# Moving the conditioning pieces, the row sums and the wide sums between the units of a one-core decoder block

## The chip, the cores and the metric

One core of one Trainium2 chip runs the whole program. The metric is the device time of one execution in microseconds (us). Matmuls run on TensorE (PE, with its weight loads shown as PEld), elementwise work on VectorE (DVE), activations and copies on ScalarE (ACT), a little on GpSimd (POOL); all transfers from memory are issued by SyncE (SP).

## The reference, cut to what matters

```
mod = silu(c) @ w_ada + b_ada;  shift, scale, gate = split(mod, 3)
h = rms_norm(x, norm1_w) * (1 + scale) + shift            # 256 tokens x 2048
q,k | v | o | z | i,f | u | B | C | zb | gA | gB = split(h @ w_in + b_in)
h_a = rms_norm(sigmoid(o) * mlstm(q, k, v, i, f)) * silu(z);   y_a = h_a @ w_proj_a
h_b = B * conv3(C * u) * silu(zb);                             y_b = h_b @ w_proj_b
x = x + gate * ((sigmoid(gA) * y_a + sigmoid(gB) * y_b) @ w_out)
out = rms_norm(x, normf_w)
```

Everything is float32; a product is made of three matmuls of a rounded head and a rest of each operand (two for the weights' rest against the head of h alone in the "wide" columns).

## The kernel before, in words

All weights stream through the core once. They are cut into 418 **units** of 128 x 1024 floats (512 KB). For each unit SP loads a tile `raw`, ACT copies its head to `wh` (L288), DVE subtracts to get the rest `wl` (L294), and PE multiplies `wh` and `wl` with the head and the rest of h. The main loop over units (L863 on) runs `advance(n + 2)` first, so DVE's instruction `wl` of unit n + 2 stands before whatever unit n adds to DVE's queue; there are three `wh` and three `wl` tiles, so ACT's copy for unit n + 2 can start only when PE is through with unit n - 1.

Units 0 to 159 are the **outer** units. h is not ready at the start, so the block goes through the five outputs qk, v, o, z, gA in **visits** (`SEGMENTS`, some k of the 16 blocks of h at a time): qk in units 0-1, v 2-3, o 4-7, z 8-13, gA 14-23, then second visits v 24-35, o 36-49, qk 50-79, z 80-105, and third or last ones o 106-119, v 120-137, gA 138-159. A unit with an even number fills one half of the output (two PSUM tiles with tag `g`), the next the other half (tag `a`). At the end of a visit `outer_evac` empties the tiles: on a first visit ACT copies them, later DVE adds them to what stands in SBUF (L394 for v, o, z; L383 for qk and gA), two adds for a half. The next visit writes the same tiles, so its first unit waits for the two adds of one half and its second for those of the other. Units 160-161 are the input and forget gates, 162-193 gB, 194-321 u, C, B, zb in four column groups j (8 units each; "wide" in all of zb and in u, C, B for j > 0: PSUM tiles are double buffered there, PE does not wait for their sums), 322-385 the two projections, 386-417 the output projection.

h itself comes from 96 **pieces** of w_ada of 512 KB each, for the matrix product with silu(c), done on DVE (L247, `ada_piece`): 64 pieces for scale and shift, then 32 for the gate. After every fourth of the first 64, four small DVE operations (L255 to L258) and one on ACT and one on DVE (L241, L242) make one more block of h. `stream` is the written order of units and pieces: piece n goes before unit u as soon as `at[n] <= u` (or when h is needed). `ADA` gives the pieces for each unit: 0.82 for the first 64, 0.45 for the rest. DVE's queue and SP's queue follow that order.

Small work that has no place of its own goes into `fillers`, of which one is run at the end of each unit. After the last visit of v, o or z its row sums are put there: `row_op` adds the bias row (L417), with `row_load` (a DMA of two 512 KB tiles) as a filler of the output before. After z's fillers (which end with the load of o's row) o's come at once.

Of the kernel before, what the change touches and what calls it, by code (L numbers as in the profile page):

```python
# [19 lines left out]
AF = mybir.ActivationFunctionType  # L20
ALU = mybir.AluOpType
PSUM = bass.MemoryType.PSUM

S, D, NH, DK, DV = 256, 2048, 8, 128, 256
# [12 lines left out]
SEGMENTS = [("qk", 0, 1), ("v", 0, 1), ("o", 0, 2), ("z", 0, 3), ("gA", 0, 5), ("v", 1, 7), ("o", 2, 9),  # L37
            ("qk", 1, 16), ("z", 3, 16), ("o", 9, 16), ("v", 7, 16), ("gA", 5, 16)]

ADA = (2.0, 0.82, 0.45)  # L40
FEATURE = ("qk", "gA")
KEEP = 4
WARM = (9, 16)
# [47 lines left out]
def body(ctx: ExitStack, tc: tile.TileContext, wu, wa, xT_d, x_d, cols_d, rows_d, out_d):  # L91
# [50 lines left out]
    pieces = [(part, k, half) for k in range(16) for part in (1, 0) for half in range(2)]  # L142
    pieces += [(2, k, half) for k in range(16) for half in range(2)]
    stream = []
    at = [0.0] * 4
    for n in range(4, len(pieces)):
        at.append(ADA[0] if n == 4 else at[-1] + 1.0 / ADA[1 if pieces[n][0] < 2 else 2])
    nxt = 0
    for u in range(NU):
        v = max(u - HD, 0)  # L150
# [198 lines left out]
    fillers = deque()  # L349
# [79 lines left out]
    def outer_after(grp, last_visit):  # L429
        if not last_visit:  # L430
            return
        d = dest[grp]
        if grp in FEATURE:
            def biased(b):
                def go():
                    for i in (b, b + 1):
                        act.activation(d[:, i, :], d[:, i, :], AF.Sigmoid if grp == "gA" else AF.Identity, bias=col(grp, i))
                return go
            if grp == "qk":
                fillers.append(row_load("z"))  # L440
            (later if grp == "gA" else fillers).extend([biased(b) for b in range(0, 16, 2)])
            return
        parts = row_op(grp, grp, ALU.add)
        if grp == "v":
            vL = {}
            vH = slot("s2", [128, 2, NH, VW], "vH", F32R)
            ml["v"] = vH, vL

            def v_split(t, half):
                hs = slice(4 * half, 4 * half + 4)  # L450

                def go():
                    act.activation(vH[:, t, hs, :], d[:, t, hs, :], AF.Copy)
                    vL[t, half] = wp.tile([128, 4, VW], F32R, name=f"vL{t}{half}", tag="ada", bufs=AB)
                    dve.tensor_tensor(vL[t, half], d[:, t, hs, :], vH[:, t, hs, :].bitcast(F32), op=ALU.subtract)
                return go
            splits = [v_split(t, half) for half in range(2) for t in range(2)]
            fillers.extend(parts[:2] + [idle] + parts[2:] + [idle] + splits)
        elif grp == "o":
            for f in parts:  # L460
                fillers.extend([f, idle])
            fillers.append(row_load("v"))
            fillers.extend(activate(d.rearrange("p t (a n) -> p (t a) n", a=2), AF.Sigmoid))
        elif grp == "z":
            for f in parts:
                fillers.extend([f, idle])
            fillers.append(row_load("hn"))
            fillers.extend(activate(d.rearrange("p t (a n) -> p (t a) n", a=2), AF.Silu))
            for f in row_op("z", "hn", ALU.mult):
                fillers.extend([f, idle])  # L470
            fillers.append(row_load("o"))
# [199 lines left out]
    def wide_sum(d, grp, j, tiles):  # L671

        for b in range(4):
            act.activation(d[:, b, :], tiles[b // 2][:, b % 2, 0:S], AF.Identity, bias=col(grp, 4 * j + b))
        for i in range(2):
            dd = d[:, 2 * i:2 * i + 2, :]
            dve.tensor_tensor(dd, tiles[i][:, :, S:2 * S], dd, op=ALU.add)

    def wide_evac(grp, j, tiles):
        u, y = hb["cv"][:, 0], hb["cv"][:, 1]  # L680
        if grp == "C":
            cu = wp.tile([128, 4, S + 4], F32, name=f"cu{j}", tag="bc", bufs=2)
            pool.memset(cu[:, :, 0:4:2], 0.0)
            wide_sum(cu[:, :, 4:], grp, j, tiles)
            dve.tensor_tensor(cu[:, :, 4:], cu[:, :, 4:], u, op=ALU.mult)
            conv_fillers(cu, j)
            return
        wide_sum(u, grp, j, tiles)
        if grp == "B":
            dve.tensor_tensor(y, u, y, op=ALU.mult)  # L690
        elif grp == "zb":
            act.activation(u, u, AF.Silu)
            zb_fillers(j)

    def conv_fillers(cu, j):
        y = hb["cv"][:, 1]
        dve.tensor_copy(cu[:, :, 1:4:2], cu[:, :, S:S + 4:2])

        def conv(b):
            def go():  # L700
                dve.tensor_scalar(y[:, b, :], cu[:, b, 0:S], col("cw0", 4 * j + b), None, op0=ALU.mult)
                dve.scalar_tensor_tensor(y[:, b, :], cu[:, b, 2:S + 2], col("cw1", 4 * j + b), y[:, b, :],
                                         op0=ALU.mult, op1=ALU.add)
                dve.scalar_tensor_tensor(y[:, b, :], cu[:, b, 4:S + 4], col("cw2", 4 * j + b), y[:, b, :],
                                         op0=ALU.mult, op1=ALU.add)
            return go
        fillers.extend([conv(b) for b in range(4)])
# [17 lines left out]
    def inner_evac(grp, j, p):  # L725
        if is_wide(grp, j):
            wide_evac(grp, j, p)
            return
        p = p[0]
        pv = p.rearrange("p a (b n) -> p (a b) n", b=2)  # L730
        blocks = [4 * j + b for b in range(4)]
        js = slice(4 * j, 4 * j + 4)
        if grp == "gB":
            if j == 0:
                hb["g"] = slot("s4", [128, 16, S], "gB")
            g = hb["g"][:, js, :]
            for b in range(4):
                act.activation(g[:, b, :], pv[:, b, :], AF.Identity, bias=col("gB", blocks[b]))
        elif grp == "u":
            if j == 0:  # L740
                hb["cv"] = slot("cb", [128, 2, 4, S], "conv_tmp")
            u = hb["cv"][:, 0]
            for b in range(4):
                act.activation(u[:, b, :], pv[:, b, :], AF.Identity, bias=col("u", blocks[b]))
        elif grp == "C":
            cu = wp.tile([128, 4, S + 4], F32, name=f"cu{j}", tag="bc", bufs=2)
            u = hb["cv"][:, 0]
            pool.memset(cu[:, :, 0:4:2], 0.0)
            for b in range(4):
                dve.scalar_tensor_tensor(cu[:, b, 4:], pv[:, b, :], col("C", blocks[b]), u[:, b, :],  # L750
                                         op0=ALU.add, op1=ALU.mult)
            conv_fillers(cu, j)
        elif grp == "B":
            y = hb["cv"][:, 1]
            for b in range(4):
                dve.scalar_tensor_tensor(y[:, b, :], pv[:, b, :], col("B", blocks[b]), y[:, b, :],
                                         op0=ALU.add, op1=ALU.mult)
        elif grp == "yA":
            g = dest["gA"][:, js, :]
            dve.tensor_tensor(g, pv, g, op=ALU.mult)  # L760
        elif grp == "yB":
            g = hb["g"][:, js, :]
            dve.tensor_tensor(g, pv, g, op=ALU.mult)
            if j == 0:
                m = slot("s01", [128, 2, 16, S], "m", F32R)
                hb["mH"], hb["mL"] = m[:, 0], m[:, 1]
            a = dest["gA"][:, js, :]

            def merge():
                dve.tensor_tensor(g, g, a, op=ALU.add)  # L770

            def merge_split():
                act.activation(hb["mH"][:, js, :], g, AF.Copy)
                dve.tensor_tensor(hb["mL"][:, js, :], g, hb["mH"][:, js, :].bitcast(F32), op=ALU.subtract)
            fillers.extend([merge, merge_split])
# [87 lines left out]
    for n, (kind, grp, k, half) in enumerate(UNITS):  # L863
# [42 lines left out]
        elif kind == "inner":  # L906
# [10 lines left out]
            if half == 7:  # L917
                while fillers and grp == "u" and k == 0 and ml["started"] < NH:
                    run_fillers(1)
                if grp == "B" or (grp == "u" and k > 0):  # L920
                    run_fillers(len(fillers))
                if grp == "yA" and k == 0:
                    run_fillers(len(fillers) + len(later))
                inner_evac(grp, k, cur["g"])
                if grp == "gB" and k == 3:
                    for j in range(4):
                        gv = hb["g"][:, 4 * j:4 * j + 4, :]
                        later.append(lambda gv=gv: act.activation(gv, gv, AF.Sigmoid))
                if grp == "yA" and k == 2:
                    fillers.append(gate_broadcast)  # L930
# [97 lines left out]
```

## Time and the profile before

| what | value |
|---|---|
| median of three runs | 1175.53 us (1174.04 to 1175.81) |
| the profiled execution, device time | 1175.07 us |
| its span, first to last instruction | 1172.6 us |
| PE busy | 1148.4 us, 98% of the span |
| DVE, ACT busy | 824.7 us (70%), 584.9 us (50%) |
| granted TensorE clock, mean | 0.998 of 2.4 GHz |

The span leaves 2.5 us of the device time outside. PE is never long idle; what it loses lies in single waits, so the timeline of PE around the ends of visits tells more than the shares.

### The profile page before, as it was taken

To read this page: it belongs to the slowest core of one execution; us is meant where nothing else is said; L and a number is where in the kernel's file an instruction comes from. 1 tells how busy PE (TensorE), PEld (TensorE's weight loads), DVE (VectorE), ACT (ScalarE), POOL (GpSimd) and SP (SyncE) were. 2 spreads that over 40 slices of the span, in tenths; PEclk is the share of its full clock that TensorE was granted. 3 is DMA by queue.
4 is the path that set the end of the run, shared out by engine and by line. 5 is a ranking of instruction groups with operands and counts; after the bars stand their busy time and mean duration, and the time that the engine had idled before them with its cause. 6 is when DMAs were issued, how large, how long until landed. Compare 5 with 4: busy or idle time off the path is not lost.

```text
span 1172.6 us, 19514 instructions
## 1 busy us (share of the span) xinstructions
PE 1148.4 (98%) x7906; PEld 1074.4 (92%) x7906; DVE 824.7 (70%) x1008; ACT 584.9 (50%) x698; POOL 16.6 (1%) x26
## 2 busy tenths in 40 slices
PE   8999999999999999999999999999999999999996
PEld 7898889988888999999999899899999999999995
DVE  6989998876888966665587566666665655556466
ACT  6754344464353556445456744644544544444453
POOL 0000000000000000000000000000000000000003
PEclk9999999999999999999999999999999999999999
DMA  9999899888788855544547556656556555486662
GB/s 345 402 368 366 317 370 360 311 323 298 260 321 295 316 199 196 182 161 161 163 163 270 197 175 222 196 180 221 194 180 227 200 195 186 144 294 208 227 206 72
DMA packets 79900, 283.48 MB, mean 242 GB/s; under 512 B 10689, under 2 KB 10817, under 8 KB 79425
## 3 DMA queue, kind: packets, MB, share of 16 engines
q1 hardware_dynamic: 79810, 282.23, 68.8%
q8 instruction: 62, 1.02, 0.3%
q14 instruction: 28, 0.23, 0.1%
HBM read 280.09 MB, written 2.11 MB: 241 GB/s over the span
## 4 chain that ended last, share of the span: by engine, by line
PE 78%; DVE 5%; ACT 2%; issue 1%; DMA 1%; DVEq 0%; ACTq 0%
PE qk L322 7%; PE out L345 6%; PE z L345 5%; PE gA L322 5%; PE v L345 3%; PE o L345 2%; PE gB2g L322 2%; PE gB1g L322 2%; PE gB3g L322 2%; PE u0g L322 2%; PE yB3g L322 2%; PE yA3g L322 2%; PE yB2g L322 2%; PE yA2g L322 2%; PE yB1g L322 2%; PE yA1g L322 2%
## 5 line engine op out<-in xcount | busy, mean ns | idle before, releaser
L294 DVE TENSOR_TENSOR wl<-raw,wh 128x1024 fp32r<-128x1024 f32 x408 | 494.8, 1222 | 272.9 <-ACT wh L288 270.5
L288 ACT ACTIVATE wh<-raw 128x1024 fp32r<-128x1024 f32 x409 | 430.4, 1059 | 444.2 <-PE qk L322 44.2
L247 DVE SCALAR_TENSOR_TENSOR ada<-ada,c_b 128x1024 f32<-128x1024 f32 x96 | 116.8, 1217 | 1.7 <-DMA ada<-wa 1.7
L345 PE MATMUL o<-wh,h 128*128 128x512 f32 x256 | 66.7, 380 | 2.2 <-DVE v_ext L394 1.6
L345 PE MATMUL v<-wh,h 128*128 128x512 f32 x256 | 66.4, 379 | 1.5 <-DVE o L394 1.5
L322 PE MATMUL qk<-h,wh 128*128 128x256 f32 x512 | 63.3, 276 | 3.9 <-DVE o L394 2.4
L345 PE MATMUL z<-wh,h 128*128 128x512 f32 x256 | 66.0, 379 | 0.0
L322 PEld LDWEIGHTS qk<-h,wh 128*128 128x128 f32 x512 | 60.0, 192 | 5.0 <-ACT h L241 1.7
L322 PE MATMUL gA<-h,wh 128*128 128x256 f32 x512 | 63.0, 276 | 0.5 <-DVE v_ext L394 0.5
L322 PEld LDWEIGHTS gA<-h,wh 128*128 128x128 f32 x512 | 60.0, 192 | 1.1 <-DVE v_ext L394 0.9
L345 PEld LDWEIGHTS o<-wh,h 128*128 128x128 f32 x256 | 48.1, 189 | 10.1 <-ACT wh L288 2.0
L345 PEld LDWEIGHTS v<-wh,h 128*128 128x128 f32 x256 | 48.2, 189 | 8.6 <-ACT wh L288 1.9
L345 PEld LDWEIGHTS z<-wh,h 128*128 128x128 f32 x256 | 48.3, 189 | 6.8
L345 PE MATMUL out<-wh,m 128*128 128x512 f32 x192 | 49.5, 379 | 0.0
L345 PEld LDWEIGHTS out<-wh,m 128*128 128x128 f32 x192 | 37.7, 197 | 3.6
L345 PE MATMUL v<-wl,h 128*128 128x512 f32 x128 | 38.2, 380 | 1.7 <-DVE wl L294 1.7
L345 PE MATMUL o<-wl,h 128*128 128x512 f32 x128 | 38.2, 380 | 0.0
L345 PE MATMUL z<-wl,h 128*128 128x512 f32 x128 | 38.1, 379 | 0.0
L322 PE MATMUL gA<-h,wl 128*128 128x256 f32 x256 | 33.8, 275 | 0.0
L322 PE MATMUL qk<-h,wl 128*128 128x256 f32 x256 | 33.8, 275 | 0.0
L322 PEld LDWEIGHTS gA<-h,wl 128*128 128x128 f32 x256 | 31.2, 192 | 0.0
L322 PEld LDWEIGHTS qk<-h,wl 128*128 128x128 f32 x256 | 31.2, 192 | 0.0
(429 smaller groups left out, 2207.2 us busy)
## 6 DMA issues: line engine op xcount, KB each, us to landing
raw<-wu SPq DMA_DIRECT2D x418, 512.0 KB, 4.4
ada<-wa SPq DMA_DIRECT2D x96, 512.0 KB, 6.0
xT<-xT SPq DMA_DIRECT2D x4, 512.0 KB, 6.3
x_res<-x SPq DMA_DIRECT2D x1, 2048.0 KB, 8.4
out<-r SPq DMA_DIRECT2D x8, 256.0 KB, 3.0
z<-rows SPq DMA_DIRECT2D x2, 512.0 KB, 7.1
hn<-rows SPq DMA_DIRECT2D x2, 512.0 KB, 8.1
o<-rows SPq DMA_DIRECT2D x2, 512.0 KB, 7.5
```

What stands on the lines that cost most here:

```text
L247: dve.scalar_tensor_tensor(t, t, 1.0, c_b[:, half * 1024:half * 1024 + 1024], op0=ALU.mult, op1=ALU.mult, accum_out=acc[:, part, k, half:h ...
L288: act.activation(head[n], r, AF.Copy)
L294: dve.tensor_tensor(rest[n], r, head[n].bitcast(F32), op=ALU.subtract)
L322: pe.matmul(o, lhsT=w[:, j + 128 * b:j + 128 * b + 128], rhs=alt(block(h)), start=st and b % 2 == 0, stop=en and b % 2 == 1, skip_group_ch ...
L345: pe.matmul(o[:, b, :], lhsT=stationary(a, k, t), rhs=alt(ww[:, c0 + 512 * b:c0 + 512 * b + 512]), start=st, stop=en, skip_group_check=True)
```

## The change

Three parts. The pieces' rate becomes 0.86 a unit up to unit 78, 0.95 from 78 to 104 and 0.45 after that, and it is multiplied by 0.4 from one unit before to three units behind each place where a second or later visit ends (units 36, 50, 80, 106, 120, 138, 160). Three empty fillers go ahead of the row sums of v, o and z. In the wide groups the two DVE sums of `wide_sum`, the product behind them, the copy of the convolution's edge and the Silu become fillers, one a unit, where they were run at the end of the group at once.

```diff
-ADA = (2.0, 0.82, 0.45)
+ADA = (2.0, ((78, 0.86), (104, 0.95), (400, 0.45)))
+QUIET = (1, 3, 0.4)
...
-    at = [0.0] * 4
-    for n in range(4, len(pieces)):
-        at.append(ADA[0] if n == 4 else at[-1] + 1.0 / ADA[1 if pieces[n][0] < 2 else 2])
+    ends, seen, u = [], set(), 0
+    for grp, k0, k1 in SEGMENTS:
+        u += 2 * (k1 - k0)
+        if grp in seen:
+            ends.append(u)
+        seen.add(grp)
+    at = [0.0] * 4 + [ADA[0]]
+    while len(at) < len(pieces):
+        rate = next(r for end, r in ADA[1] if at[-1] < end)
+        if any(e - QUIET[0] <= at[-1] < e + QUIET[1] for e in ends):
+            rate *= QUIET[2]
+        at.append(at[-1] + 1.0 / rate)
...
         parts = row_op(grp, grp, ALU.add)
+        fillers.extend([idle] * 3)
...
-        for i in range(2):
-            dd = d[:, 2 * i:2 * i + 2, :]
-            dve.tensor_tensor(dd, tiles[i][:, :, S:2 * S], dd, op=ALU.add)
+
+        def add(i):
+            def go():
+                dd = d[:, 2 * i:2 * i + 2, :]
+                dve.tensor_tensor(dd, tiles[i][:, :, S:2 * S], dd, op=ALU.add)
+            return go
+        fillers.extend([add(0), add(1)])
...
-            dve.tensor_tensor(cu[:, :, 4:], cu[:, :, 4:], u, op=ALU.mult)
+            fillers.append(lambda: dve.tensor_tensor(cu[:, :, 4:], cu[:, :, 4:], u, op=ALU.mult))
+            fillers.append(lambda: conv_edge(cu))
...
         if grp == "B":
-            dve.tensor_tensor(y, u, y, op=ALU.mult)
+            fillers.append(lambda: dve.tensor_tensor(y, u, y, op=ALU.mult))
         elif grp == "zb":
-            act.activation(u, u, AF.Silu)
+            fillers.append(lambda: act.activation(u, u, AF.Silu))
             zb_fillers(j)
+
+    def conv_edge(cu):
+        dve.tensor_copy(cu[:, :, 1:4:2], cu[:, :, S:S + 4:2])
...
-                if grp == "B" or (grp == "u" and k > 0):
+                if grp in ("u", "C", "B", "zb") and k > 0 or grp == "B":
                     run_fillers(len(fillers))
```

**The order on DVE at the end of v's second visit.** Before, from `wl` of unit 36 on (a row with `ada` is a piece, `v_ext<-v` are the adds that free PSUM):

```order
L294 TENSOR_TENSOR wl_1141<-raw_1016,wh_1140 128x1024
L247 SCALAR_TENSOR_TENSOR ada_1035,acc<-ada_1035,c_b 128x1024
L394 TENSOR_TENSOR v_ext<-v_929,v_ext 128x4x256
L394 TENSOR_TENSOR v_ext<-v_930,v_ext 128x4x256
L294 TENSOR_TENSOR wl_1164<-raw_1037,wh_1163 128x1024
L247 SCALAR_TENSOR_TENSOR ada_1058,acc<-ada_1058,c_b 128x1024
L394 TENSOR_TENSOR v_ext<-v_952,v_ext 128x4x256
L394 TENSOR_TENSOR v_ext<-v_953,v_ext 128x4x256
```

The same place on DVE of the change, from the last piece before it on:

```order
L258 SCALAR_TENSOR_TENSOR ada_1038,acc<-ada_1038,c_b 128x1024
L305 TENSOR_TENSOR wl_1143<-raw_1040,wh_1142 128x1024
L405 TENSOR_TENSOR v_ext<-v_932,v_ext 128x4x256
L405 TENSOR_TENSOR v_ext<-v_933,v_ext 128x4x256
L305 TENSOR_TENSOR wl_1165<-raw_1042,wh_1164 128x1024
L405 TENSOR_TENSOR v_ext<-v_955,v_ext 128x4x256
L405 TENSOR_TENSOR v_ext<-v_956,v_ext 128x4x256
```

Both pieces have left the stretch between `wl` of unit 36 and the last add. The ends of o's (unit 50), qk's (80) and v's last visit (138) read alike in the change: no piece stands there.

**The order on DVE at the end of o's last visit** (unit 120), where the change is smaller. Before, from `wl` of unit 120 on (`z<-z,hn` is a row product of z's fillers):

```order
L294 TENSOR_TENSOR wl_3279<-raw_3158,wh_3278 128x1024
L247 SCALAR_TENSOR_TENSOR ada_3160,acc<-ada_3160,c_b 128x1024
L394 TENSOR_TENSOR o<-o_3038,o 128x1024
L394 TENSOR_TENSOR o<-o_3039,o 128x1024
L417 TENSOR_TENSOR z<-z,hn_3192 128x1024
L294 TENSOR_TENSOR wl_3301<-raw_3178,wh_3300 128x1024
L394 TENSOR_TENSOR o<-o_3059,o 128x1024
L394 TENSOR_TENSOR o<-o_3060,o 128x1024
```

The same place on DVE of the change:

```order
L305 TENSOR_TENSOR wl_3293<-raw_3176,wh_3292 128x1024
L258 SCALAR_TENSOR_TENSOR ada_3178,acc<-ada_3178,c_b 128x1024
L405 TENSOR_TENSOR o<-o_3059,o 128x1024
L405 TENSOR_TENSOR o<-o_3060,o 128x1024
L305 TENSOR_TENSOR wl_3317<-raw_3198,wh_3316 128x1024
L405 TENSOR_TENSOR o<-o_3079,o 128x1024
L405 TENSOR_TENSOR o<-o_3080,o 128x1024
```

The row product is gone from here (it now stands behind `wl` of unit 123), the piece is not. The end of z's last visit (106) has one piece ahead of the adds in the change too, where before it stood ahead of the second pair.

**The order on DVE behind the first wide group, zb with j = 0** (the units are those of u, j = 1). Before, from `wl` of unit 227 on:

```order
L294 TENSOR_TENSOR wl_6714<-raw_6575,wh_6713 128x1024
L677 TENSOR_TENSOR conv_tmp<-zb0g,conv_tmp 128x512
L677 TENSOR_TENSOR conv_tmp<-zb0a,conv_tmp 128x512
L717 TENSOR_TENSOR conv_tmp<-conv_tmp 128x1024
L294 TENSOR_TENSOR wl_6746<-raw_6599,wh_6745 128x1024
L722 TENSOR_TENSOR hbL<-conv_tmp,hbH 128x1024
L294 TENSOR_TENSOR wl_6772<-raw_6623,wh_6771 128x1024
```

The same place on DVE of the change:

```order
L305 TENSOR_TENSOR wl_6714<-raw_6575,wh_6713 128x1024
L691 TENSOR_TENSOR conv_tmp<-zb0g,conv_tmp 128x512
L305 TENSOR_TENSOR wl_6743<-raw_6599,wh_6742 128x1024
L691 TENSOR_TENSOR conv_tmp<-zb0a,conv_tmp 128x512
L305 TENSOR_TENSOR wl_6768<-raw_6623,wh_6767 128x1024
L305 TENSOR_TENSOR wl_6791<-raw_6647,wh_6790 128x1024
L736 TENSOR_TENSOR conv_tmp<-conv_tmp 128x1024
L305 TENSOR_TENSOR wl_6814<-raw_6671,wh_6813 128x1024
L741 TENSOR_TENSOR hbL<-conv_tmp,hbH 128x1024
```

At most one of these operations now stands between two `wl`; on ACT the Silu, which the product L717 waits for, has moved behind two more copies `wh`.

## Rows read from the trace of the kernel before

**Rows 1.** The page: busy time of PE, and GB/s in 40 slices of the span.
```profile
PE 1148.4 (98%) x7906; PEld 1074.4 (92%) x7906; DVE 824.7 (70%) x1008; ACT 584.9 (50%) x698; POOL 16.6 (1%) x26
...
GB/s 345 402 368 366 317 370 360 311 323 298 260 321 295 316 199 196 182 161 161 163 163 270 197 175 222 196 180 221 194 180 227 200 195 186 144 294 208 227 206 72
```

**Rows 2.** The waits of PE: who for whom, us in total, times, longest.
```profile
PE qk L322 <- DVE o L394: 2.4, 4, 1.0
PE v L345 <- DVE wl L294: 1.7, 1, 1.7
...
PE o L345 <- DVE v_ext L394: 1.6, 1, 1.6
PE v L345 <- DVE o L394: 1.5, 1, 1.5
...
PE o L345 <- DVE z L394: 0.4, 1, 0.4
```

**Rows 3.** Timeline of DVE, end of v's second visit (start us, us, instruction, [idle before]).
```profile
112.20 1.22 DVE L294 TENSOR_TENSOR wl<-raw,wh 128x1024 fp32r<-128x1024 f32 x1 [0.22 <-ACT wh L288]
113.35 1.22 DVE L247 SCALAR_TENSOR_TENSOR ada<-ada,c_b 128x1024 f32<-128x1024 f32 x1
...
114.49 2.35 DVE L394 TENSOR_TENSOR v_ext<-v,v_ext 128x1024 f32<-128x1024 f32 x2
116.76 1.21 DVE L294 TENSOR_TENSOR wl<-raw,wh 128x1024 fp32r<-128x1024 f32 x1
...
119.03 2.35 DVE L394 TENSOR_TENSOR v_ext<-v,v_ext 128x1024 f32<-128x1024 f32 x2
```

**Rows 4.** Timeline of PE at the same place: units 36 and 37 begin.
```profile
116.05 0.59 PE L345 MATMUL o<-wh,h 128*128 128x512 f32 x2
...
118.20 0.59 PE L345 MATMUL o<-wh,h 128*128 128x512 f32 x2
120.40 0.67 PE L345 MATMUL o<-wh,h 128*128 128x512 f32 x2 [1.60 <-DVE v_ext L394]
```

**Rows 5.** Timeline of PE, end of o's second visit to unit 52.
```profile
153.71 0.59 PE L345 MATMUL o<-wh,h 128*128 128x512 f32 x2
...
161.99 1.06 PE L322 MATMUL qk<-h,wl 128*128 128x256 f32 x8
162.88 1.95 PE L322 MATMUL qk<-h,wh 128*128 128x256 f32 x16
```

**Rows 6.** Timeline of DVE, end of z's last visit, second half.
```profile
307.06 2.35 DVE L394 TENSOR_TENSOR z<-z,z 128x1024 f32<-128x1024 f32 x2
```

**Rows 7.** Timeline of DVE in v's last visit: the first row sum of o.
```profile
370.07 1.23 DVE L417 TENSOR_TENSOR o<-o,o 128x1024 f32<-128x1024 f32 x1 [4.03 <-DMA o<-rows]
```

**Rows 8.** Timeline of PE, end of v's last visit: units 138 and 140 begin.
```profile
392.88 0.61 PE L322 MATMUL gA<-h,wh 128*128 128x256 f32 x4
...
399.41 0.83 PE L322 MATMUL gA<-h,wh 128*128 128x256 f32 x6
```

**Rows 9.** Timeline of PE in the wide groups: first matmuls of u (j = 1), and of yA.
```profile
652.19 0.60 PE L330 MATMUL u1g<-h,wh 128*128 128x512 f32 x2
...
653.50 0.60 PE L330 MATMUL u1g<-h,wh 128*128 128x512 f32 x2
...
906.83 0.61 PE L322 MATMUL yA0g<-haH,wh 128*128 128x256 f32 x4
```

**Rows 10.** Timeline of DVE behind zb, j = 0.
```profile
656.14 1.23 DVE L717 TENSOR_TENSOR conv_tmp<-conv_tmp 128x1024 f32<-128x1024 f32 x1 [1.68 <-ACT conv_tmp L692]
657.28 1.22 DVE L294 TENSOR_TENSOR wl<-raw,wh 128x1024 fp32r<-128x1024 f32 x1
```

**Rows 11.** Busy time of the engines early on: PE, PEld, DVE, ACT, POOL, clock, DMA share, GB/s.
```profile
30.00:40.00 10.00, 9.76 (x45) 8.23 (x45) 9.59 (x18) 8.40 (x10) 0.00 (x0) 1.00 1.03 409
```

**Rows 12.** Timelines of DVE and of PE where gA ends and gB begins.
```profile
455.22 2.35 DVE L294 TENSOR_TENSOR wl<-raw,wh 128x1024 fp32r<-128x1024 f32 x2
...
457.48 0.61 PE L322 MATMUL gB0g<-h,wl 128*128 128x256 f32 x4
```

More of the change, by code (lines that the diff above doesn't have):

```diff
@@ L689, in wide_evac @@
         if grp == "B":
-            dve.tensor_tensor(y, u, y, op=ALU.mult)
+            fillers.append(lambda: dve.tensor_tensor(y, u, y, op=ALU.mult))
         elif grp == "zb":
-            act.activation(u, u, AF.Silu)
+            fillers.append(lambda: act.activation(u, u, AF.Silu))
             zb_fillers(j)
+    def conv_edge(cu):
+        dve.tensor_copy(cu[:, :, 1:4:2], cu[:, :, S:S + 4:2])
     def conv_fillers(cu, j):
         y = hb["cv"][:, 1]
-        dve.tensor_copy(cu[:, :, 1:4:2], cu[:, :, S:S + 4:2])
         def conv(b):
@@ L751, in inner_evac @@
                                          op0=ALU.add, op1=ALU.mult)
+            conv_edge(cu)
             conv_fillers(cu, j)
```

## The prediction

> **What bounds the kernel now.** First the page's busy times: PE works 98% of the span [rows 1], so a change can only win what PE loses in single waits, or lose by making more. Then the list of PE's waits: behind the start-up nearly all of them are on DVE, and on two kinds of DVE work, adds that empty PSUM (L394) and `wl` [rows 2]. Then the timelines of PE and DVE at the places where these waits lie. The reader is to see there that DVE is not too slow on the average; for one or two units at the end of a visit it has a line of operations in front of the one that PE needs.
>
> A wait costs more than its idle time, so I price each place by starts of matmuls. Twelve matmuls of 512 columns make a token unit: 116.05 to 118.63 (118.20 and two more of 0.216), 2.59 us [rows 4]. A feature unit (qk, gA) is 24 of 256 columns: eight take 162.88 - 161.99 = 0.89, the unit 2.68 [rows 5].
>
> - v's second visit ends: unit 37 should start at 118.63 and starts at 120.40, **1.8 us** [rows 4].
> - o's second visit ends: unit 50 should start at 154.14 (153.71 + 0.43), unit 52 two feature units later at 159.50; it starts at 162.88, **3.4** [rows 5].
> - z's ends: idle 0.4 [rows 2] and 0.17 of refill (in rows 4 the idle of 1.60 costs 1.77), **0.6**.
> - o's last visit ends: idle 1.5 and refill, **1.7** [rows 2].
> - in v's last visit PE waits 1.7 for a `wl` [rows 2], with refill **1.9**. That `wl` stood behind o's first row sum, which waited 4.03 for its row to land [rows 7].
> - v's last visit ends: units 138 and 139 take 399.41 - 392.88 = 6.53 instead of 5.36, **1.2** [rows 8].
> - the wide groups: half a unit takes 653.50 - 652.19 = 1.31, the 96 units from u (j = 1) to yA 251.5; they take 906.83 - 652.19 = 254.6, **3.1** [rows 9].
>
> **Part one: pieces away from the ends.** DVE's prices are starts to next starts [rows 3]: `wl` 1.15, a piece 1.14 (113.35 to 114.49), two adds 2.27, `wl` and a piece 2.27 (116.76 to 119.03). Count from the start of unit 34 (116.05 - 5.18 = 110.87). `wl` of unit 36 starts at 1.33. With both pieces the first add of the second half starts at 8.16, ends at 9.3, and the matmul begins 0.23 after that end (120.17 to 120.40); PE wants it at 7.77. One piece less: 8.4 against 7.77, a loss of 0.6. This can be checked: at z's end one piece stands ahead of the adds, they begin at 307.06 [rows 6], and the loss is the 0.6 above. No piece: 7.25 against 7.77, no loss and half a us to spare.
>
> The order says which case each end is. v's second visit: none left, 1.8 won; what arrears the pieces ahead leave on DVE are covered up to that half us. o's second visit: none left, but qk takes both tiles of a half within its first 0.45 us, so it is the second add that counts: 8.4 plus some arrears against 8.3; I keep 0.3 of the 3.4 and win 3.1. qk's end lost nothing and gets lighter. z's end: one piece before, one after, nothing won. o's last: one piece stays, the row product goes; 0.6 of 1.7 stays, 1.1 won. v's last: none left, second add against feature units as at unit 50 but without arrears, 0.1 stays, 1.1 won. Sum **7.1**; bounds: 5.5 if each cleared end keeps 0.4 more, 8.1 if all waits at these four ends go.
>
> What the denser stretches cost. Units 87 to 102 get a piece in every unit. DVE then has 2.27 of 2.59 a unit there and no other work: cover holds, 0. DMA moves two tiles of 0.524 MB a unit; at the 409 GB/s that it held early [rows 11] that is 2.56 of 2.59. Also 0, with little cover: `raw` is six deep and is the only reserve. The blocks of h come up to two units later than before (the last one's rest stands right behind `wl` of unit 78, which is two units ahead of PE): 0.
>
> **Part two: row sums three units later.** They cost the same, elsewhere: o's row is now loaded four units (10.4 us) before the first sum instead of one, which is more than the 4.03 that lacked, so the 1.9 goes, **1.9** won. z's first row sum leaves the crowded unit 107. The price is at the far end: 9 fillers more in a row (three outputs) move the split of v (`vL`, 1.14 each, as the other subtractions of this size) from units 148-151 to 157-159 and beyond; the order has one of the four between the two pairs of gA's last adds. `wl` of unit 162 starts at 455.22, is done some 1.2 later, and PE reads it at 457.48 [rows 12]: 1.1 to spare, 1.14 and the hand-over to pay, so **0.2 lost** (bounds 0 and 0.6).
>
> **Part three: wide sums one a unit.** In the first group DVE waits for the Silu until 656.14, and `wl` of unit 228 stands behind that product until 657.28 and is done some 1.2 later, at 658.5 [rows 10]; PE would be in unit 228 from 657.43 (652.19 + 2 x 2.62) and want it four matmuls of 0.216 later, at 658.3. In the change one operation at most stands between two `wl`, and the Silu (with its table load) comes after two `wh`. `advance` begins two units (5.24 us) ahead, which is enough for the copy, `wl` and one such operation (1.2 each), and the sums are not urgent since PSUM is double buffered there. All of the **3.1** goes (bounds 1.5 and 3.1; the low one if half of these waits are ACT's).
>
> **Sum.** 7.1 + 1.9 - 0.2 + 3.1 = 11.9 us. From the profiled execution's 1175.07 this gives 1163.2; the median of the runs is 0.5 higher than that execution, so 1163.2 to 1163.7. I say **1163.3**.
>
> **A rule weighed.** In rows 11 DMA moves 409 GB/s for 10 us. The Trainium skill ("DMA: Bandwidth & Descriptors", section "Where 436 GB/s comes from") says that for transfers from HBM to SBUF the HBM side binds, at about 358 GB/s. By that the 32 tiles of units 87 to 102 would take 46.9 us instead of the 41.4 that PE needs, and without any reserve the time would be 5.5 higher, an estimate of 1168.8. The trace's own rate speaks against it; the rival below takes its price from rows alone.
>
> **Rivals.**
> 1. *The ends keep more than I reckon*: arrears on DVE of one more piece at each of the three ends reckoned clear of it (36, 50, 138), 0.6, 1.2 and 0.6, and the split of v 0.4 more: 2.8 less, **1166**. For it: at the 0.86 rate `wl` and the pieces alone fill 2.1 of 2.59 on DVE [rows 3], and the small operations of each block of h come on top. Against: the quiet stretch takes it off just there.
> 2. *The wide waits stay*, since on ACT the copies `wh` and not the sums on DVE are late: 3.1 less, **1166.4**. For it: DVE's row waits for ACT's Silu [rows 10]. Against: the Silu too now comes after the copies.
> 3. *DMA becomes the bound in units 87 to 102; slower than before.* The page's slices 8 to 11 (205 to 322 us) show only 311, 323, 298 and 260 GB/s [rows 1]. If that is what it can give there and not what is asked, 32 tiles (16.8 MB) at 298 take 56.3 instead of 41.4: 14.9 lost against 11.9 won, **1178**. It decides the sign at 315 GB/s (16.8 MB in 41.4 + 11.9). Against: 1.45 tiles in 2.59 us are 294 GB/s, which is what the kernel asked for there. A milder form, at 368 as in two of the first slices [rows 1], loses 4.2: **1167.5**.
> 4. *The change does nothing at the ends because PE then waits for something just behind*, `wh` from ACT above all: 7.1 less, **1170.4**. Against: ACT is idle half of the span [rows 1].
>
> **How the numbers follow.** Forecast 0.70 (its own range 1161 to 1165), rival 1 0.11, rival 2 0.05, rival 3 0.04 in the strong form and 0.05 in the mild one, rival 4 0.03, and 0.02 for more won than reckoned. The range 1160.3 to 1167.8 holds the forecast, rivals 1 and 2 and the mild form of 3. About 0.2%, 2.4 us, is what a measurement of this kernel can tell. Below 1173.2 lie all cases but the strong form of 3: faster 0.93, within 0.03, slower 0.04.
>
> **What would show it.** Right: unit 37, 50 to 52 and 138 to 140 start on time on PE; about 0.6 stays at the ends of z and of o's last visit; no wait of DVE for o's row; the 96 wide units take 251.5; DMA at 390 to 409 GB/s in units 87 to 102 with no wait of ACT for `raw`. Wrong: new waits of PE on `wl` between units 87 and 105, or ACT waiting there for DMA (rival 3); waits on L405, the new number of L394, at the cleared ends (rival 1); wide groups still above 20.96 us each (rival 2); a wait at gB's first `wl` of over 0.6.

## The result, and the profile after

The changed kernel takes 1163.2 us (median of 4 runs, 1162.76 to 1164.05), the kernel before beside it 1175.05 (1174.04 to 1175.81): a ratio of 0.9889, 95% interval 0.9872 to 0.9906, 1.1% faster. The forecast was 1163.3. The profiled execution took 1162.83, with a span of 1161.0 us at a granted clock of 0.998; before it was 1175.07 and 1172.6. So 11.6 us went inside the span, and 0.6 in what lies around it (2.5 before, 1.8 after). Two executions of the runs below stand apart, 4557.97 us in e4_silu and 1698.35 us in e10_after (the changed kernel itself, at a granted clock of 0.654); their cause is open, and the medians and ratios below are those of the other executions.

The page of the changed kernel, its busy times and its GB/s in 40 slices, beside [rows 1]:

```profile
PE 1144.1 (99%) x7906; PEld 1075.0 (93%) x7906; DVE 824.5 (71%) x1008; ACT 584.9 (50%) x698; POOL 16.6 (1%) x26
...
GB/s 347 367 404 367 333 330 361 355 353 408 298 274 290 237 209 182 198 150 149 160 181 271 198 203 200 197 206 202 195 206 191 212 191 191 151 290 209 225 203 73
```

DVE and ACT are as busy as before: no work was taken out, it only stands elsewhere. PE's busy time fell by 4.3 of the 11.6: part of the time lost counts as busy, as in the 0.67 us of two matmuls behind a wait, for which 0.59 is usual. PE's waits, beside [rows 2]:

```profile
PE qk L333 <- ACT h L252: 2.2, 1, 2.2
...
PE v L356 <- DVE o L405: 0.9, 2, 0.6
PE gB0g L333 <- ACT wh L299: 0.5, 1, 0.5
PE o L356 <- DVE z L405: 0.4, 1, 0.4
```

L405 is the L394 of before. Of the adds that held up PE in [rows 2] only those behind o's last visit are left, with 0.9 in two waits instead of 1.5 in one, and z's, which were forecast to stay. The 1.7 for a `wl` in v's last visit is gone.

The starts of units on PE, beside [rows 4, 5, 8, 9]:

```profile
116.40 0.59 PE L356 MATMUL o<-wh,h 128*128 128x512 f32 x2
...
118.56 1.03 PE L356 MATMUL o<-wh,h 128*128 128x512 f32 x4
...
152.66 1.95 PE L333 MATMUL qk<-h,wh 128*128 128x256 f32 x16
...
158.19 1.95 PE L333 MATMUL qk<-h,wh 128*128 128x256 f32 x16
...
337.96 0.67 PE L356 MATMUL v<-wh,h 128*128 128x512 f32 x2 [0.32 <-DVE o L405]
...
341.35 0.67 PE L356 MATMUL v<-wh,h 128*128 128x512 f32 x2 [0.57 <-DVE o L405]
...
385.46 1.95 PE L333 MATMUL gA<-h,wh 128*128 128x256 f32 x16
...
390.85 1.95 PE L333 MATMUL gA<-h,wh 128*128 128x256 f32 x16
...
643.66 0.60 PE L341 MATMUL u1g<-h,wh 128*128 128x512 f32 x2
...
895.18 0.61 PE L333 MATMUL yA0g<-haH,wh 128*128 128x256 f32 x4
```

Unit 36 now starts at 116.40, and unit 37 at the third of the four matmuls from 118.56, so at 118.99: 2.59, with no wait. Units 50 and 51 take 158.19 - 152.66 = 5.53 instead of 5.36, so 0.17 is left. At 337.96 and 341.35 stand the two waits of o's last end. Units 138 and 139 take 390.85 - 385.46 = 5.39. The 96 wide units take 895.18 - 643.66 = 251.5, to the tenth what was forecast.

To put all places on one scale I take each unit's length, from its first matmul to the next unit's. What a place loses is its excess over the 2.59, 2.68 or 2.62 us of an undisturbed unit:

| place | lost before | forecast to stay | lost after |
|---|---|---|---|
| v's second end (units 36, 37) | 1.8 | 0 | 0 |
| o's second end (49 to 51) | 3.4 | 0.3 | 0.2 |
| z's end (106) | 0.6 | 0.6 | 0.6 |
| behind it (108) | 0.3 | not priced | 0 |
| o's last end (119 to 121) | 1.8 | 0.6 | **1.4** |
| row of o (130) | 2.0 | 0 | 0 |
| v's last end (138, 139) | 1.2 | 0.1 | 0 |
| gB's begin (162 and 168) | 0.9 at 168 | 0.2 more | 0.3 at 162, 0.7 at 168 |
| wide groups | 3.1 | 0 | 0 |
| start: first matmul of unit 0 at | 21.04 | 21.04 | 21.33 |

So one line is off by more than a few tenths: o's last visit. These are its rows in the trace of the changed kernel, ACT first, then DVE:

```profile
329.90 1.06 ACT L299 ACTIVATE wh<-raw 128x1024 fp32r<-128x1024 f32 x1 [1.53 <-PE o L356]
330.98 1.28 ACT L434 ACT_TABLE_LOAD   x1
332.27 1.06 ACT L434 ACTIVATE z<-z 128x1024 f32<-128x1024 f32 x1
333.23 1.04 ACT L299 ACTIVATE wh<-raw 128x1024 fp32r<-128x1024 f32 x1
```

```profile
334.31 1.23 DVE L305 TENSOR_TENSOR wl<-raw,wh 128x1024 fp32r<-128x1024 f32 x1 [2.09 <-ACT wh L299]
335.45 1.22 DVE L258 SCALAR_TENSOR_TENSOR ada<-ada,c_b 128x1024 f32<-128x1024 f32 x1
336.59 0.08 DVE L258 DVE_READ_ACCUMULATOR ada<-ada,c_b 128x1 f32 x1
336.59 2.35 DVE L405 TENSOR_TENSOR o<-o,o 128x1024 f32<-128x1024 f32 x2
338.86 1.21 DVE L305 TENSOR_TENSOR wl<-raw,wh 128x1024 fp32r<-128x1024 f32 x1
339.99 2.34 DVE L405 TENSOR_TENSOR o<-o,o 128x1024 f32<-128x1024 f32 x2
```

The copies `wh` of an o unit begin 2.59 apart (the one before began at 329.90, so this one was due at 332.49). z's Silu, for which ACT first loads a table, stands in front of it, and it begins at 333.23, 0.74 late. DVE has nothing to do for 2.09 us and then does `wl`, one piece and the adds, all of it as much later. Before, the Silus ran three units earlier (the table load ahead of the copy of unit 117) and hit no end. They follow z's row sums, which part two moved. The experiments test whether this is the cause.

The dense stretch of pieces held. Busy times of the engines in two windows over units 87 to 102 (us, then PE, PEld, DVE, ACT, POOL, clock, DMA share, GB/s):

```profile
251.00:272.00 21.00, 21.00 (x99) 18.40 (x98) 19.23 (x26) 9.25 (x10) 0.00 (x0) 1.00 1.01 389
272.00:293.00 21.00, 21.00 (x99) 18.39 (x98) 18.08 (x24) 8.46 (x9) 0.00 (x0) 1.00 1.03 409
```

PE is busy throughout, at DMA rates of 389 and 409 GB/s. The rule weighed in the prediction, the 358 GB/s of the Trainium skill ("DMA: Bandwidth & Descriptors", section "Where 436 GB/s comes from"), does not hold here; the measurement decides. There was less in hand than the absence of waits suggests: the time from a `raw` tile's landing to its use fell from 7.9 us (unit 87) to 1.4 (units 101 to 103).

### The profile page after: what moved, and what is told of

It reads as the page before. It is cut to its first block, busy times and chain, and to the rows that moved or that the text cites. A ratio compares the mean times of both kernels' runs of the same rounds, so it can differ in the third digit from the quotient of the medians.

```text
span 1161.0 us, 19524 instructions
## 1 busy us (share of the span) xinstructions
PE 1144.1 (99%) x7906; PEld 1075.0 (93%) x7906; DVE 824.5 (71%) x1008; ACT 584.9 (50%) x698; POOL 16.6 (1%) x26
## 4 chain that ended last, share of the span: by engine, by line
PE 93%; DVE 4%; ACT 1%; DMA 1%; issue 1%; SPq 0%; DVEq 0%; ACTq 0%
PE gA L333 7%; PE qk L333 7%; PE z L356 7%; PE v L356 6%; PE out L356 6%; PE o L356 6%; PE gB1g L333 2%; PE gB2g L333 2%; PE gB3g L333 2%; PE u0g L333 2%; PE C0g L333 2%; PE yB3g L333 2%; PE yA3g L333 2%; PE yB2g L333 2%; PE yA2g L333 2%; PE yB1g L333 2%
```

## The experiments

Each was timed beside the kernel before; the comparison with the changed kernel by units is that of the profiled executions, from the first matmul of unit 0 to the first of unit 408 (an output unit), so that the start-up, which differs by up to 2.7 us between executions, stays out of it. The changed kernel is 11.9 below the kernel before on that measure, and e10_after, the changed kernel executed again, differs from it by 0.02.

| kernel | median us | ratio to before, 95% | by units |
|---|---|---|---|
| e1_pieces | 1169.5 | 0.9944 (0.9922 to 0.9966) | -6.4 to before |
| e2_sums | 1172.8 | 0.9969 (0.9959 to 0.9978) | -2.7 to before |
| e3_wide | 1171.9 | 0.9965 (0.9947 to 0.9982) | -3.2 to before |
| e4_silu | 1163.0 | 0.9886 (0.9866 to 0.9905) | -0.7 to after |
| e5_clear | 1162.0 | 0.9875 (0.9860 to 0.9890) | -1.8 to after |
| e6_best | 1160.9 | 0.9865 (0.9849 to 0.9882) | -2.0 to after |
| e7_dense | 1165.9 | 0.9907 (0.9892 to 0.9922) | +2.7 to after |
| e8_noquiet | 1170.3 | 0.9948 (0.9934 to 0.9963) | +7.0 to after |
| e9_warm | 1161.6 | 0.9879 (0.9862 to 0.9895) | -0.5 to after |
| e10_after | 1162.5 | 0.9890 (0.9874 to 0.9907) | 0.0 to after |
| e11_best | 1160.7 | 0.9878 (0.9863 to 0.9892) | -0.5 to after |
| e12_warm2 | 1161.0 | 0.9870 (0.9854 to 0.9887) | -1.5 to after |

**The three parts one by one.** e1_pieces is the kernel before with the new `ADA`, `QUIET` and the loop over `ends`:

```diff
-ADA = (2.0, 0.82, 0.45)
+ADA = (2.0, ((78, 0.86), (104, 0.95), (400, 0.45)))
+QUIET = (1, 3, 0.4)
```

> The kernel before with part one alone (the new rates and the quiet stretches). Theory (each end is a sum of operations in front of the add that PE needs, and the three parts do not touch each other): v's second end 1.8 won, o's second end 3.1 to 3.2, v's last end 1.1; o's last end keeps its 1.7 because the piece and the row product still stand there and z's Silus are early, the wait for o's row keeps its 1.9, the wide groups their 3.1. Sum 6.1, about 1169.0. Rival (what cleared the ends is that the row sums went away from them): under 4 won, over 1171. Second rival (the denser pieces push the row sums too, so that the row of o lands in time): 8 won, about 1167.

Measured by units: 1.8 won at v's second end, 3.2 at o's, 1.1 at v's last; o's last end and the wide groups as before; of the wait for o's row 0.35 won. The first theory, within 0.3 us. The row sums stand where they stood, so they had nothing to do with the ends that were cleared.

e2_sums is the kernel before with part two's line alone:

```diff
         parts = row_op(grp, grp, ALU.add)
+        fillers.extend([idle] * 3)
```

> The kernel before with part two alone (three idle fillers ahead of each group of row sums). Theory: o's row is loaded early enough, 2.0 won at unit 130; the crowded unit behind z's end 0.3 won; o's last end falls from 1.8 to about 1.4, since the row product leaves it but z's Silus, three units later, now make the copy of that unit late; gA's end 0.3 lost. Sum 2.4, about 1172.7. Rival (the Silus do not matter, the row product alone does): o's last end falls to 0.6, sum 3.2, about 1171.9, and no DVE wait for ACT at that end.

Measured by units: 2.0 won at unit 130, 0.31 at 108, 0.41 at o's last end, 0.26 lost at 162 and 0.23 of it given back at 168. DVE's list of waits has no wait for o's row any more. At o's last end the list of PE's waits of e2_sums reads

```profile
PE v L345 <- DVE o L394: 0.9, 2, 0.6
```

as in the changed kernel, where the kernel before had one wait of 1.5. This is the loss of the changed kernel, made by part two alone: the row product left, and the late copy came in its place.

e3_wide is the changed kernel with the old `ADA`, the old `at` and without the idle fillers:

```diff
-ADA = (2.0, ((78, 0.86), (104, 0.95), (400, 0.45)))
-QUIET = (1, 3, 0.4)
+ADA = (2.0, 0.82, 0.45)
...
-        fillers.extend([idle] * 3)
```

> The changed kernel without parts one and two, so part three alone. Theory: the waits in the wide groups are sums in front of the copies; 3.1 won, about 1172.0, the 96 wide units take 251.5, the ends lose as before. Rival (half of what the wide groups won came from the earlier end of the work on h and the row sums, or the matmuls there are bound by ACT): 1.5 won, about 1173.5.

Measured: in the wide groups just the units that differ between before and after, by the same amounts, 3.1 in all; the ends lose as before. Together the three parts alone give 6.4 + 2.7 + 3.2 = 12.3 by units, the change gives 11.9: apart from the 0.35 of o's row, which parts one and two both count, they add up.

**o's last end.** e4_silu moves z's sums and Silus alone one unit earlier:

```diff
-        fillers.extend([idle] * 3)
+        fillers.extend([idle] * {"z": 2, "o": 4, "v": 3}[grp])
```

> The changed kernel with two idle fillers instead of three ahead of z's sums and four instead of three ahead of o's, so that z's sums and Silus alone come one unit earlier. Theory (the table load and the first Silu hold up the copy wh of unit 120, which puts 0.75 us on the piece and the adds behind its wl): with the Silus ahead of the copy of unit 119 instead, where DVE has time, o's last end falls from 1.38 to about 0.57, 0.8 won, about 1162.4, and everything else stays. Rival (the piece there alone costs 1.4): no change, 1163.2.

ACT and PE at o's last end in e4_silu:

```profile
329.48 1.28 ACT L434 ACT_TABLE_LOAD   x1
330.77 1.06 ACT L434 ACTIVATE z<-z 128x1024 f32<-128x1024 f32 x1
331.73 1.04 ACT L299 ACTIVATE wh<-raw 128x1024 fp32r<-128x1024 f32 x1
332.68 1.04 ACT L434 ACTIVATE z<-z 128x1024 f32<-128x1024 f32 x1
333.62 1.04 ACT L299 ACTIVATE wh<-raw 128x1024 fp32r<-128x1024 f32 x1
```

```profile
PE v L356 <- DVE o L405: 0.4, 1, 0.4
```

The first rows are ACT's timeline, the last is PE's wait at this end. The late copy is now that of unit 119 (331.73); that of unit 120 begins at 333.62, in front of unit 120's start at 338.56 by as much as elsewhere. The piece is still there, and o's last end falls from 1.38 to 0.68, about what z's end loses with one piece and a copy on time. The rival is out. The median of the runs does not show the 0.7: unit 0 began 1.1 later in this profiled execution, and 0.06% is less than the interval.

e5_clear leaves the Silus and takes the piece away:

```diff
+    for e in ends:
+        for n in range(len(at)):
+            if e < at[n] <= e + 2:
+                at[n] = e + 2.5
```

> The changed kernel with a rule that puts no piece into the two units of an end (pieces due there come two units later); two pieces move, one at z's end and one at o's last end. Theory (a piece in front of the adds costs 0.6 at an end that has nothing else, and more where the copy is late): z's end falls from 0.57 to 0, o's last end from 1.38 to 0.1 or 0.2, since the adds then begin 1.14 earlier. Sum 1.8, about 1161.4. Rival (at o's last end the late copy alone makes the loss): only z's 0.57 and at most 0.4 more won, about 1162.4.

DVE at o's last end in e5_clear:

```profile
334.75 1.22 DVE L309 TENSOR_TENSOR wl<-raw,wh 128x1024 fp32r<-128x1024 f32 x1 [2.09 <-ACT wh L303]
335.89 2.35 DVE L409 TENSOR_TENSOR o<-o,o 128x1024 f32<-128x1024 f32 x2
...
339.29 2.35 DVE L409 TENSOR_TENSOR o<-o,o 128x1024 f32<-128x1024 f32 x2
```

The copy is as late as in the changed kernel (DVE waits the same 2.09), but without the piece the adds follow `wl` at once, and only about 0.2 is left at this end; z's end goes to 0. So the end pays for the late copy and for the piece, and neither alone makes the 1.38: the copy without the piece costs 0.2, the piece without the late copy 0.7, both 1.4. An end has about one small stretch of slack, and the second thing that comes late is paid in full. The half microsecond that the prediction found to spare (7.25 against 7.77) gives these figures as an estimate: 0.74 - 0.52 = 0.2 for the copy, 1.14 - 0.52 = 0.6 for the piece, and 0.74 + 1.14 - 0.52 = 1.4 for both.

e6_best does both and also drops the idle fillers ahead of v's sums:

```diff
+        fillers.extend([idle] * {"z": 2, "o": 4, "v": 0}[grp])
```

> The changed kernel with that rule, with two idle fillers ahead of z's sums, four ahead of o's and none ahead of v's. Theory: z's end and o's last end lose nothing (0.57 and 1.38 won), and the split of v is done ahead of gA's last adds, so that the 0.26 at gB's begin goes too. Sum 2.2, about 1161.0. Rival (what is taken off these places turns up at the next one, because DVE has no time left around them): under 1 won.

Measured: 0.57 and 1.38 won. At gB's begin unit 162 won 0.26 and unit 168 lost 0.24, the mirror image of what part two does there. The copy that unit 169 waits for ends 19.6 us behind the first matmul of unit 162 in the kernel before, the changed one and this one alike, whether unit 162 itself takes 2.68 or 2.94; so what is lost in between is given back. The term "0.2 lost" was right at its place and worth nothing.

**What DMA bears.** e7_dense raises the dense rate:

```diff
-(104, 0.95)
+(104, 1.2)
```

> The changed kernel with a rate of 1.2 pieces a unit instead of 0.95 between units 78 and 104. DVE then has 1.15 + 1.2 x 1.14 = 2.5 of 2.59 a unit, DMA 2.2 tiles of 0.524 MB, 1.15 MB in 2.59 us, 445 GB/s asked. Theory (DMA has no more than the 409 GB/s seen early): a unit takes 2.82 for DMA, 0.23 too much over some 17 units, 3.9 behind in all, of which the six raw buffers hide 1.4 to 2.9 us; 1 to 2.5 lost in the stretch with ACT waiting for DMA, and 1.4 won at o's last end where no piece is left; 1162.8 to 1164.3. Rival (this stretch is bound by what is asked, not by DMA): the pieces come at 1.2 a unit, no ACT wait for raw, 1.4 won, about 1161.9. Rival (DMA gives here only what the page's slices showed before, 298 to 323): 10 or more lost.

ACT's wait for DMA between 240 and 300 us, and the busy times of two windows:

```profile
ACT wh L299 <- DMA raw<-wu: 30.0, 19, 2.8
```

```profile
280.00:290.00 10.00, 9.69 (x45) 8.48 (x46) 9.27 (x13) 4.24 (x4) 0.00 (x0) 1.00 1.03 410
290.00:300.00 10.00, 9.43 (x43) 7.57 (x42) 9.23 (x13) 4.24 (x4) 0.00 (x0) 1.00 1.03 409
```

Asked for 445 GB/s, DMA gives 409 to 410; from unit 89 on each `raw` is used 0.1 us after it lands, and from unit 98 on PE pays: 3.1 us in units 98 to 105. At qk's last end and z's 0.8 more is lost (units 80, 81 and 106), and 1.16 is won at o's last end, where no piece is left. The theory of a ceiling at 409 is right in kind and was sized too low (1 to 2.5 in the stretch, 1162.8 to 1164.3 in all, where 3.1 and 1165.9 were measured). The rival of 298 to 323 GB/s is out: that was what had been asked for.

**What the quiet stretch is worth.** e8_noquiet:

```diff
-QUIET = (1, 3, 0.4)
+QUIET = (1, 3, 1.0)
```

> The changed kernel with the new rates but without the quiet stretches (the factor 0.4 is 1.0). Pieces come back to the ends of v's second visit (one), o's second (two and four small operations), qk's last (two), z's (one and two small operations); none is left at o's last end. Theory (the quiet stretch wins the ends): 0.6, 2.0 and 0 to 0.6 lost, 0.4 lost at z's end, 1.4 won at o's last end: 1.6 to 2.2 slower than the changed kernel, about 1165. Rival (the rates do it, the quiet stretches nothing): 1.4 faster, about 1161.8.

It is slower by 7.0 by units, three to four times what I expected: 1.1 at v's second end, 5.8 at o's second, 0.7 at qk's last, 0.4 at z's; 1.2 is won at o's last. DVE and then PE at o's second end, and the busy times there:

```profile
150.85 1.22 DVE L305 TENSOR_TENSOR wl<-raw,wh 128x1024 fp32r<-128x1024 f32 x1
151.99 1.21 DVE L258 SCALAR_TENSOR_TENSOR ada<-ada,c_b 128x1024 f32<-128x1024 f32 x1
...
153.13 2.35 DVE L405 TENSOR_TENSOR o<-o,o 128x1024 f32<-128x1024 f32 x2
155.40 1.21 DVE L305 TENSOR_TENSOR wl<-raw,wh 128x1024 fp32r<-128x1024 f32 x1
156.53 1.21 DVE L258 SCALAR_TENSOR_TENSOR ada<-ada,c_b 128x1024 f32<-128x1024 f32 x1
...
158.65 2.35 DVE L405 TENSOR_TENSOR o<-o,o 128x1024 f32<-128x1024 f32 x2
```

```profile
154.49 0.68 PE L333 MATMUL qk<-h,wh 128*128 128x256 f32 x4 [0.90 <-DVE o L405]
...
160.01 0.68 PE L333 MATMUL qk<-h,wh 128*128 128x256 f32 x4 [1.98 <-DVE o L405]
```

```profile
160.00:162.00 2.00, 1.63 (x8) 1.45 (x9) 2.00 (x2) 0.22 (x1) 0.00 (x0) 0.66 0.95 373
162.00:164.00 2.00, 2.00 (x12) 2.00 (x11) 2.00 (x4) 0.00 (x0) 0.00 (x0) 0.50 0.13 47
164.00:166.00 2.00, 2.00 (x19) 2.00 (x19) 1.64 (x3) 1.06 (x1) 0.00 (x0) 0.99 0.15 20
```

Two things were missing from my sum. First, `wl` of unit 50 starts at 150.85, at the start of unit 49 (150.84) on PE; in the changed kernel it starts 1.16 ahead of that (148.91 against 150.07). The pieces in the units ahead had left DVE that much in arrears, so the end starts late before its own pieces count. Secondly, behind the idle times of 0.90 and 1.98 the granted clock is 0.50 (1.2 instead of 2.4 GHz) for some 3.4 us, and twelve matmuls of 256 columns take 2.72 (161.05 to 163.77) where the twelve from 155.53 took 1.44. In the prediction's terms this is rival 1 (arrears), which the quiet stretch holds off. The rival that the rates do it is out for v's second end and o's second end. It holds for v's last end, where e8_noquiet loses as little as the changed kernel (0.03). DVE there:

```profile
388.16 1.23 DVE L305 TENSOR_TENSOR wl<-raw,wh 128x1024 fp32r<-128x1024 f32 x1 [0.23 <-ACT wh L299]
389.31 2.35 DVE L405 TENSOR_TENSOR v_ext<-v,v_ext 128x1024 f32<-128x1024 f32 x2
391.57 1.21 DVE L305 TENSOR_TENSOR wl<-raw,wh 128x1024 fp32r<-128x1024 f32 x1
392.70 2.35 DVE L405 TENSOR_TENSOR v_ext<-v,v_ext 128x1024 f32<-128x1024 f32 x2
```

No piece is left for this end: DVE does the last of the 96 pieces while PE is in unit 104 here and in unit 130 in the changed kernel, but in unit 143 in the kernel before.

**The start.** e9_warm puts six warm-up matmuls of 128x128 between those for `c` and the sum of squares, into e6_best, and e12_warm2 also makes the 16 behind it 24; e10_after and e11_best are the changed kernel and e6_best again on the same chip.

```diff
-WARM = (9, 16)
+WARM = (9, 24)
...
+    keep_warm(6)
     square(0)
```

> The kernel of e6_best with six more warm-up matmuls of 128x128 between those for c and the sum of squares. In the profiled executions in which PE stood idle 2.3 us or more ahead of the sum of squares, the granted clock was half for the next 3 us and unit 0 began at 22.2 to 23.0; where it stood idle 1.3 to 1.7 it kept full clock and unit 0 began at 20.3 to 21.3. Theory (the idle time before it halves the clock, and that is most of the spread between executions): idle stays under 1.5 us, clock 1.00 from 10 to 15 us, unit 0 begins at or before 21.5, the median is 0.5 to 1.2 lower than that of e11_best, and the runs lie closer together. Rival (the start is late because DVE and ACT are, and the clock only follows): no change of the median.

> The changed kernel itself, beside the other two: about 1163.2.

> The kernel of e6_best again, beside the changed kernel on the same chip. By the units of its first profile it is 2.0 less than the changed kernel (0.57 at z's end, 1.38 at o's last end; the 0.26 at gB's begin comes back five units later), about 1161.2.

> The kernel of e9_warm with 24 instead of 16 warm-up matmuls behind the sum of squares, which fill 1.9 of the 2.2 us that PE stood idle ahead of unit 0 there. In e9_warm the clock stayed at 1.00 before that idle time and halved behind it, so that units 0 and 1 took 1.6 more. Theory (the clock follows the idle time on PE): no stretch below 1.00 up to 25 us, unit 0 begins at 21.2 to 21.5 and takes 2.86; 1.0 to 1.6 less than e9_warm and e11_best, about 1159.8. Rival (the clock falls without that idle time too, or the warm-up matmuls make unit 0 late): no change, 1161.

Behind the long idle times that the expectation names, unit 0 began at 22.0 to 23.0 and not at 22.2 to 23.0 (e3_wide began at 22.00). In the first profiled e6_best PE idled 2.7 ahead of the sum of squares, and unit 0 began at 22.97; in e9_warm it idles 0.6 there, keeps full clock, and unit 0 begins at 21.21. But in e9_warm (and in e11_best, where the first idle time happened to be 1.8) the clock then fell after the idle time in front of unit 0, and units 0 and 1 took 1.6 more. PE's wait and the window 20 to 25 us of e9_warm:

```profile
PE qk L338 <- ACT h L257: 2.2, 1, 2.2
```

```profile
20.00:25.00 5.00, 3.79 (x23) 3.79 (x24) 4.39 (x6) 3.19 (x5) 0.00 (x0) 0.76 1.04 411
```

In e12_warm2 that idle time is 0.3, the window 20 to 25 has a clock of 1.00, and units 0 and 1 take 2.86 and 2.68:

```profile
PE qk L338 <- ACT h L257: 0.3, 1, 0.3
```

```profile
20.00:25.00 5.00, 4.70 (x41) 4.51 (x40) 4.39 (x6) 3.61 (x5) 0.00 (x0) 1.00 1.03 410
```

So in these profiles the clock fell only behind idle times, as the theory says, but not behind each: the changed kernel idles 2.2 in front of unit 0 and keeps 1.00. e12_warm2 has the shortest span of the profiled executions, 1159.4 (0.6 of the gain goes again at unit 6, where PE waits for a block of h). The gain that was forecast for the median did not come, in either run. e9_warm was to be 0.5 to 1.2 below e11_best and is 0.9 above it, 1161.6 against 1160.7. e12_warm2 was to be 1.0 to 1.6 below and has 1161.0, the rival's figure; it ran on another chip, and the ratios to the kernel before (0.9870, and 0.9878 and 0.9879 for the other two) lie within each other's intervals. The profiled executions of e6_best and e11_best took 1162.38 each, where their other executions took 1160.27 to 1161.10. So the profiled start-up may not be the usual one; that stays open. e11_best against e10_after gives 1.8 us by medians, near the 2.0 of the first profiles by units, though the two intervals overlap.

## Why the prediction was right, point by point

**What bounds the kernel.** Right: PE is busy 99% of the span, and all that was won came out of single waits.

**v's second end, o's second end, v's last end.** Right in mechanism and size: 1.8, 3.2 and 1.1 won against 1.8, 3.1 and 1.1. e1_pieces gives these numbers by part one alone. e8_noquiet shows which half of part one makes them: without the quiet stretch v's second end loses 1.1 and o's second 6.0, but v's last end nothing more. So there the raised rates alone did it, because the pieces have run out by then. The prediction said that no piece is left there, but not why. z's end kept its 0.6 with its one piece, and e5_clear shows that it was the piece.

**o's last end: the term that was mis-sized.** "One piece stays, the row product goes; 0.6 of 1.7 stays, 1.1 won": 0.4 was won. I followed the moved row sums on DVE, up to the split of v at gA's end, and left out what hangs on them on ACT. z's Silus come behind its sums; with them a table load of 1.28 and a Silu of 1.06 landed in front of the copy of the very unit in which the piece stands. e2_sums makes this loss alone, and e4_silu takes it away by moving the Silus a unit.

**o's row.** 2.0 won against 1.9. That the crowded unit behind z's end gets lighter was said, but not priced: 0.3.

**gA's end and gB's begin.** 0.26 lost against 0.2, and 0.24 of it given back at unit 168, which I did not see; e6_best shows the same exchange the other way round.

**The wide groups.** 3.1 against 3.1, by e3_wide alone as well. Rival 2 is out.

**The dense stretch.** Priced at 0, and it cost 0: no wait of ACT for DMA, 389 and 409 GB/s. e7_dense shows that rival 3's mechanism exists: with 445 GB/s asked it loses 3.1 us, at the kernel's 409 none; where between the two it begins was not measured.

**The sum.** The errors cancelled: 0.7 less at o's last end and 0.3 at the start-up, 0.3 more behind z's end, some 0.2 at gB, and 0.6 more outside the span. That the forecast lies within 0.1 of the median says less than the table by places.

## What to carry to other kernels

When an operation is moved in a queue of fillers, follow everything that comes behind it in that queue on every engine, not only on its own: the late table load stood on ACT, the price was paid on DVE and PE. An end of a visit with little slack bears one late thing, and the second is paid in full (0.2 and 0.7 alone, 1.4 together), so price coincidences, not single costs. And where background work is paced by a rate, let it pause ahead of the places where the foreground comes in bursts: the same rates without the pause gave back 7.0 of 11.9 us.

## What was unexpected of the hardware

Short idle times of PE can cost twice: behind waits of 0.90 and 1.98 us at o's second end in e8_noquiet the granted clock was 0.50 for some 3.4 us. In the start-ups it was 0.50 for some 3.4 us behind idle times of 2.3 to 2.8 (e2_sums to e6_best) and kept 1.00 behind 1.3 to 1.8; behind 2.2 in front of unit 0 it kept 1.00 in the changed kernel and fell in e9_warm (0.76 over 20 to 25 us). So the length of one idle time does not settle it, and these runs don't show what else does.

DMA on this one core held 409 to 411 GB/s for over 40 us (e7_dense, 251 to 293 us and on to 300) and gave no more when more was asked.
